# Later operand copies in attention, a later norm of the next rows, and a y part made inside the last down-projection

## The chip, the cores and the metric

The kernel runs on one core of one Trainium2 chip, as one launch. The metric is device time: the median of three timed runs is 3419.69 us (3419.29 to 3424.39). Beside it stands one profiled execution, from which all views come.

## The reference

One layer of a hybrid decoder trunk over 2048 tokens and 16 meta tokens in front, width 1024, all in float32:

```
u      = rms_norm(h) @ w_in + b_in          # 5 parts: attention, RWKV, two gates
y_attn = sliding-window attention (128) with sinks, partial rotary q and k,
         meta tokens as global keys          # 8 query heads, 2 key heads of 64
y_rwkv = RWKV-7 time mixing                  # state update per token, group norm, output gate
h      = h + (g1 * (y_attn @ w_br_attn) + g2 * (y_rwkv @ w_br_rwkv)) @ w_o
f      = rms_norm(h)
h      = h + (silu(f @ w_gate) * (f @ w_up)) @ w_down
out    = rms_norm(h)                         # without the meta tokens
```

## The kernel before

A float32 operand is split in two parts, the first of which ScalarE writes by a copy and the second of which VectorE writes by a subtraction (`chunk`, `split_of`, `Acts`, `Ys.make`); a product is three matmuls on the parts (`mm3`), 128 x 512 each. All TensorE work is of this kind or small matmuls of the two mixers.

The tokens are worked in four blocks of 512. `phase_a(b)` norms a block and makes 37 chunks of the input projection in the order of a list `ORDER`; the chunks go to DRAM (`po` to `proj_d` and `gate_d`). `phase_c(b)` takes a block through the two branch products (`pb`, from the mixers' results `y`, eight parts `ya`), the output product (`ph_o`), a norm, the feed-forward products (`pg`, `pu`, then `ph_d` with `mg_g`) and the final norm, which `finished(t, hf)` does for each of eight pieces of the last down-projection (`ph_d_l`). The program's order is phase A of all blocks, then phase C of all blocks.

Between the products the mixers run: `tick()` (L1016) steps generators, one of attention (`attn(ti)`, L914, 16 tiles of 128 tokens) and up to two of the RWKV units (i, j); each product yields its estimated time, and a tick is due for each third of 4 us of it, an attention step in each third tick. Before phase C of block b the main loop ticks until all mixers' work of the block is in the program (`open_`, L1047).

In an attention tile, q, k and their rotary partners `qr`, `kr` are loaded, GpSimd multiplies by cosine and sine and adds (L934 to L936 for q, L883 to L885 for k: tiles `q`, `kl`), `set_keys` copies the keys on ScalarE to `kw` (L873) and subtracts on VectorE, and `parts(g)` does the same for the queries, `qs` (L944, L945). Scores are `psS`, probabilities go through `pp` and `ptt` to `py`. GpSimd also runs the recurrence of an RWKV unit, 31 pairs of rows `pr` and `xv` (L761, L763), and the power of each norm (`rstd_end`, L232); SyncE fetches `lt` and `xv` for a unit and all weights `wr`.

What sets the order. TensorE's rows stand strictly in the program's order. On ScalarE, VectorE, GpSimd and SyncE a scheduler chooses among the rows of a window by an estimated timeline; `HA`, `HV` issue with high priority, and `late(r)` fixes row r behind the row that was written before it on its engine. A tile takes a buffer of its tag when one comes free: `ld` has 4 buffers (loads `tg`, `yl`, outputs `po`), `act` 8, `tmp` 2, `h` 1 (the block's rows `h`, or the next rows `x`).

In `phase_a`, `rows_of(b + 1)` (L338) at `ORDER[20]` loads the next block's rows `x` and norms them: Squares `jk`, sums `ss_a`, then products. In `phase_c`, `Ys(b)` gives the parts of `y`; the first use, `y[0]`, makes all eight (load `yl`, copy and subtraction `ya`).

Of the kernel before, what the change touches and what calls it, by code (L numbers as in the profile page):

```python
# [21 lines left out]
AF = mybir.ActivationFunctionType  # L22
ALU = mybir.AluOpType
# [4 lines left out]
P = 128  # L28
# [4 lines left out]
NB = SEQ // TB  # L33
# [9 lines left out]
ORDER = [6, 7, 8, 9, 10, 11, 4, 5, 0, 1, 2, 3] + list(range(12, 37))  # L43
# [35 lines left out]
def layer(ctx, tc, x, meta, w_in, w_br, w_o, w_gate, w_up, w_down, w2a, a2, g2, vecs, sinks, gfin,  # L79
          consts, rope, out):  # L80
    nc = tc.nc
    V, A, G, S = nc.vector, nc.scalar, nc.gpsimd, nc.sync
# [20 lines left out]
    def late(r):  # L103

        tc.keep_in_program_order(r)
        return r
# [70 lines left out]
    mhalf = cp.tile([P, 8], F32, name="mhalf")  # L177
# [24 lines left out]
                    return f(*p, **k)  # L202
            return g

    HA, HV = High(A), High(V)


    def chunk(src, name, pin=False):
# [14 lines left out]
        T.matmul(ps, lh, rl, start=False, stop=False)  # L223
        T.matmul(ps, ll, rh, start=False, stop=stop)

    def rstd_half(ss, src, rows, hf, junk):
        HA.activation(junk[:rows, :512], src[:, hf * 512:(hf + 1) * 512], AF.Square, accum_out=ss[:rows, hf:hf + 1])

    def rstd_end(ss, rows):
        HV.tensor_add(ss[:rows, 2:3], ss[:rows, 0:1], ss[:rows, 1:2])  # L230
        HV.tensor_scalar(ss[:rows, 2:3], ss[:rows, 2:3], 1.0 / D, 1e-6, op0=ALU.mult, op1=ALU.add)
        G.tensor_tensor(ss[:rows, 3:4], ss[:rows, 2:3], mhalf[:rows, 0:1], op=ALU.pow)  # L232
        return ss[:rows, 3:4]

    def junk(name):
# [2 lines left out]
    def stat(name):  # L238
        return dn.tile([P, 4], F32, tag="stat", bufs=8, name=f"ss_{name}")

    def rstd_of(src, rows, name, junk):
        ss = stat(name)
        for hf in range(2):
            rstd_half(ss, src, rows, hf, junk)
        return rstd_end(ss, rows)

    class Acts:
# [87 lines left out]
    nxt = [None]  # L335
    emitted = [set() for _ in range(NB)]

    def rows_of(b):  # L338
        rows = []
        xa = dn.tile([P, 4, D], F32, tag="h", name=f"x_{b}")  # L340
        for t in range(4):
            with tc.high_priority():
                late(S.dma_start(xa[:, t], x[b * TB + t * P:b * TB + (t + 1) * P, :]))
        for t in range(4):
            xt = xa[:, t]
            jk = dn.tile([P, 512], F32, tag="tmp", bufs=2, name=f"jk_{b}_{t}")
            r = rstd_of(xt, P, f"a{b}_{t}", jk)
            rows.append((xt[:, :512], xt[:, 512:]))
            HV.tensor_scalar(rows[t][0], rows[t][0], r, None, op0=ALU.mult)
            HA.activation(rows[t][1], rows[t][1], AF.Copy, scale=r)  # L350
        return Acts(rows, "g_mix", f"u{b}")

    def phase_a(b):
        u = nxt[0] or rows_of(b)
        nxt[0] = None
        rest = None
        ws = []
        mid = lambda ci: lambda: ws.append(chunk(w_in[ci], f"in_{b}_{ci}", True))
        for n_, ci in enumerate(ORDER):
            w = ws.pop(0) if ws else chunk(w_in[ci], f"in_{b}_{ci}")  # L360
            if ci == ORDER[20] and b < NB - 1:
                nxt[0] = rows_of(b + 1)
            if ci == ORDER[-1] and b == NB - 1:
                nxt[0] = Ys(0)
            yield from in_chunk(b, ci, u, w, nxt[0] if ci == ORDER[-1] else None, mid(ORDER[n_ + 1]) if b == 0 and n_ < 2 else None)
            if rest:
                rest()
                rest = None
            if b == 0 and ci == ORDER[0]:
                load_rest()  # L370
                meta_norm()
            if b == 0 and ci in META_CH:
                rest = meta_chunk(ci, w)
            else:
                emitted[b].add(ci)
# [29 lines left out]
    class Ys:  # L405
# [14 lines left out]
                self.make()  # L420
            return self.made[k]

        def make(self):
            k = len(self.made)
            if self.early:
                yl = self.early[k // 2][:, k % 2]
            else:
                yl = self.load(dn.tile([P, 1, 512], F32, tag="ld", bufs=4, name=f"yl_{self.b}_{k}"), k, 1)[:, 0]
            a = dn.tile([P, 2, 512], F32R, tag="act", bufs=8, name=f"ya_{self.b}_{k}")
            HA.activation(a[:, 0], yl, AF.Copy)  # L430
            HV.tensor_sub(a[:, 1], yl, f32(a[:, 0]))
            self.made.append(a)

# [6 lines left out]
    def phase_c(b):  # L440
# [6 lines left out]
        for f in range(KT):  # L447
# [24 lines left out]
        rows, st = [], []  # L472
# [41 lines left out]
        sf = []  # L514

        def finished(t, hf):
            if hf == 0:
                sf.append(stat(f"o{b}_{t}"))
            rstd_half(sf[t], h[:, t], P, hf, junk(f"o{b}_{t}_{hf}"))
            if hf:  # L520
                r = rstd_end(sf[t], P)
                for q, e in ((0, S), (1, A)):
                    c = slice(512 * q, 512 * q + 512)
                    if t < 3 and q == 0:
                        HA.activation(h[:, t, c], h[:, t, c], AF.Copy, scale=r)
# [340 lines left out]
    kw = cp.tile([P, 2, 2, 272], F32R, name="kw")  # L866
    MC = slice(P, P + NM)

    def set_keys(k, cols):
        for g in range(2):  # L870
            gb = slice(64 * g, 64 * g + 64)
            for d in (gb, slice(64 - 64 * g, 128 - 64 * g)):
                A.activation(kw[d, g, 0, cols], k[gb], AF.Copy)  # L873
                V.tensor_sub(kw[d, g, 1, cols], k[gb], f32(kw[gb, g, 0, cols]))

    vzs = [cp.tile([P, 3, 64], F32, name=f"vz{q}") for q in range(2)]
# [4 lines left out]
    def roped(o, src, rot, cs, w, name):  # L881

        G.tensor_mul(src, src, cs[:, 0])  # L883
        G.tensor_mul(rot, rot, cs[:, 1])
        G.tensor_add(o, src, rot)  # L885
# [28 lines left out]
    def attn(ti):  # L914
# [7 lines left out]
        q = mx.tile([P, 4, P], F32, tag="q", bufs=1, name=f"q_{ti}")  # L922
# [12 lines left out]
        G.tensor_mul(qr, qr, b4(1))  # L935
        G.tensor_add(q, q, qr)  # L936
        roped(kl[:, 0], kl[:, 0], kr[:, 0], cs, P, ti)
        set_keys(kl[:, 0], own)

        def parts(g):  # L940

            gb, ob = slice(64 * g, 64 * g + 64), slice(64 - 64 * g, 128 - 64 * g)
            qs = mx.tile([P, 4, P], F32R, tag="q0", bufs=1, name=f"qs_{ti}_{g}")
            A.activation(qs[gb], q[gb], AF.Copy)  # L944
            V.tensor_sub(qs[ob], q[gb], f32(qs[gb]))  # L945
            return qs

        qs = parts(0)
# [6 lines left out]
        for g in range(2):  # L955
            gb = slice(64 * g, 64 * g + 64)
# [89 lines left out]
    def open_(b):  # L1046
        return (any(u[3] <= b for u in units) or any((i or 0) // 2 <= b for i, _ in todo_r)  # L1047
                or any((t or 0) // 4 <= b for t in todo_a))

    credit = 0.0  # L1050
    for ph, b in [("a", b) for b in range(NB)] + [("c", b) for b in range(NB)]:
        while ph == "c" and open_(b):
            tick()
        for us in (phase_a if ph == "a" else phase_c)(b):
            credit += us
            while credit >= STEP / TURNS:
                credit -= STEP / TURNS
                tick()
# [119 lines left out]
```

## Time and profile before

| | us |
|---|---|
| median of 3 timed runs | 3419.69 |
| profiled execution, its own time | 3412.06 |
| its span | 3410.3 |
| TensorE busy (share of the span) | 3263.3 (96%) |
| VectorE busy | 1929.6 (57%) |
| ScalarE busy | 1499.4 (44%) |
| GpSimd busy | 1004.8 (29%) |

The mean granted clock of TensorE is 0.984 of full speed. The page's chain of work that ended last is PE 46%, issue 20%, POOL 20%, DMA 7%: where TensorE waits, the chain often runs through GpSimd's recurrence rows and the loads between them. Busy time of the other engines matters only where TensorE waits for one of them; the table of waits and the timelines at those places show where.

### The profile page before, as it was taken

The numbers are of one execution on the slowest core, as the hardware profiler recorded it, in microseconds if no ns is written. First come the engines' busy times: TensorE is split into PE (matmuls) and PEld (weight loads), VectorE is DVE, ScalarE is ACT, GpSimd is POOL, SyncE is SP. The second block draws the span as 40 slices with busy tenths as digits, with TensorE's granted clock in tenths as the row PEclk, the third lists the DMA queues.
The fourth block names the chain that finished last, engine by engine and source line by source line (L and its number), as shares of the span: only waits on it lengthen the run. The fifth ranks groups of instructions, "written<-read, shape, count | busy, mean of one in ns | idle before, by whom it ended". The sixth has DMA issues, their size and how long they took to land.

```text
span 3410.3 us, 47506 instructions
## 1 busy us (share of the span) xinstructions
PE 3263.3 (96%) x16909; PEld 2682.7 (79%) x16909; DVE 1929.6 (57%) x3860; ACT 1499.4 (44%) x3101; POOL 1004.8 (29%) x2290
## 2 busy tenths in 40 slices
PE   8999999999999989999989899999989999999999
PEld 6887778887778777778868788887777888778887
DVE  3344445554544775656667656657655555764455
ACT  4455456554544564445443533434353333432222
POOL 0133333343333343333343244334333341100000
PEclk9999999999999999999989999999999999999999
DMA  4544444454544433333244333335332332522222
GB/s 144 160 144 129 161 133 134 140 157 133 163 131 139 142 103 103 97 91 102 85 139 151 95 102 101 90 98 168 122 95 85 102 94 90 196 96 94 98 99 99
DMA packets 227027, 409.50 MB, mean 120 GB/s; under 512 B 61829, under 2 KB 120581, under 8 KB 226790
## 3 DMA queue, kind: packets, MB, share of 16 engines
q1 hardware_dynamic: 192854, 356.98, 34.5%
q10 hardware_dynamic: 32352, 47.31, 4.0%
q8 instruction: 133, 2.18, 0.3%
q0 software_dynamic: 1584, 2.18, 0.2%
q14 instruction: 104, 0.85, 0.1%
HBM read 346.29 MB, written 60.04 MB: 119 GB/s over the span
## 4 chain that ended last, share of the span: by engine, by line
PE 46%; issue 20%; POOL 20%; DMA 7%; DVE 4%; ACT 2%; SPq 1%; POOLq 0%; ACTq 0%; DVEq 0%
PE pi L93 15%; POOL pr L761 9%; POOL xv L763 8%; PE pg L93 7%; PE pu L93 7%; PE ph_d L93 5%; PE ch L93 2%; PE pb L93 1%; PE ph_o L93 1%; PE py L93 1%; DMA lt<-lt_d 1%; DMA wr_in<-in_w_in 1%; DMA xt_d<-xv 1%; DVE h L202 1%; PE ph_d_l L93 1%
## 5 line engine op out<-in xcount | busy, mean ns | idle before, releaser
L93 PE MATMUL pi<-act_u,wh_in 128*128 128x512 f32 x2368 | 764.1, 404 | 2.3 <-DVE act_u L202 2.1
L761 POOL TENSOR_TENSOR pr<-xv,lt 128x124 f32<-128x124 f32 (+30 forms) x992 | 398.1, 401 | 584.6 <-DMA lt<-lt_d 468.9
L93 PEld LDWEIGHTS pi<-act_u,wh_in 128*128 128x128 f32 x2368 | 425.3, 190 | 83.2 <-issue 5.7
L93 PE MATMUL pi<-act_u,wl_in 128*128 128x512 f32 x1184 | 465.6, 393 | 0.6 <-DVE wl_in L202 0.6
L93 PE MATMUL pg<-act_f,wh_g 128*128 128x512 f32 x1408 | 453.6, 403 | 7.2 <-DVE act_f L202 7.1
L93 PE MATMUL pu<-act_f,wh_u 128*128 128x512 f32 x1408 | 446.7, 398 | 0.0
L93 PE MATMUL ph_d<-wh_d,mg_g 128*128 128x512 f32 x1280 | 428.4, 399 | 16.4 <-DVE th L202 13.6
L763 POOL TENSOR_TENSOR xv<-xv,pr 128x124 f32<-128x124 f32 (+30 forms) x992 | 380.9, 384 | 76.5
L93 PEld LDWEIGHTS pg<-act_f,wh_g 128*128 128x128 f32 x1408 | 256.5, 190 | 57.5 <-DVE act_f L202 9.8
L93 PEld LDWEIGHTS pu<-act_f,wh_u 128*128 128x128 f32 x1408 | 257.5, 189 | 50.3 <-issue 1.5
L93 PEld LDWEIGHTS ph_d<-wh_d,mg_g 128*128 128x128 f32 x1280 | 241.7, 189 | 69.8 <-DVE th L202 15.2
L202 DVE TENSOR_TENSOR wl_in<-wr_in,wh_in 128x1024 fp32r<-128x1024 f32 x148 | 187.0, 1264 | 184.4 <-PE pi L93 126.8
L93 PE MATMUL pg<-act_f,wl_g 128*128 128x512 f32 x704 | 277.6, 394 | 0.0
L93 PE MATMUL pu<-act_f,wl_u 128*128 128x512 f32 x704 | 275.8, 392 | 0.0
L93 PEld LDWEIGHTS pi<-act_u,wl_in 128*128 128x128 f32 x1184 | 223.4, 189 | 51.0 <-DVE wl_in L202 1.0
L93 PE MATMUL ph_d<-wl_d,mg_g 128*128 128x512 f32 x640 | 250.4, 391 | 0.0
L850 POOL TENSOR_TENSOR gst<-gst,mhalf 128x4 f32<-128x4 f32 x32 | 36.1, 1128 | 707.2 <-DVE gst L849 656.8
L202 DVE SCALAR_TENSOR_TENSOR h<-ph_d,h 128x512 f32<-128x512 f32 x320 | 216.5, 685 | 49.1 <-PE ph_d L93 48.1
L202 ACT ACTIVATE wh_g<-wr_g 128x1024 fp32r<-128x1024 f32 x88 | 93.3, 1060 | 220.3 <-PE ph_d L93 81.5
L202 ACT ACTIVATE wh_in<-wr_in 128x1024 fp32r<-128x1024 f32 x148 | 155.8, 1053 | 56.1 <-DMA wr_in<-in_w_in 47.5
L202 DVE TENSOR_TENSOR wl_d<-wr_d,wh_d 128x1024 fp32r<-128x1024 f32 x80 | 99.3, 1242 | 133.1 <-PE pg L93 53.6
L202 DVE TENSOR_TENSOR wl_u<-wr_u,wh_u 128x1024 fp32r<-128x1024 f32 x88 | 108.4, 1232 | 115.5 <-issue 54.2
(358 smaller groups left out, 5940.3 us busy)
## 6 DMA issues: line engine op xcount, KB each, us to landing
wr_in<-in_w_in SPq DMA_DIRECT2D x148, 512.0 KB, 3.8
wr_g<-in_w_gate SPq DMA_DIRECT2D x88, 512.0 KB, 3.6
wr_u<-in_w_up SPq DMA_DIRECT2D x88, 512.0 KB, 3.4
wr_d<-in_w_down SPq DMA_DIRECT2D x80, 512.0 KB, 3.3
proj_d<-po ACTq DMA_DIRECT2D x84, 256.0 KB, 2.5
gate_d<-po ACTq DMA_DIRECT2D x64, 256.0 KB, 2.2
lt<-lt_d SPq DMA_DIRECT2D x32, 512.0 KB
wr_br<-in_w_br SPq DMA_DIRECT2D x32, 512.0 KB, 5.1
```

The lines of the kernel that those rows point to most:

```text
L93: r = f(*p, **k)
L202: return f(*p, **k)
L761: G.tensor_mul(pr[:, :, :n_], xv[:, :, r:r + 1].to_broadcast([P, 4, n_]), lt[:, r, r + 1:].unsqueeze(1).to_broadcast([P, 4, n_]))
L763: G.tensor_add(xv[:, :, r + 1:], xv[:, :, r + 1:], pr[:, :, :n_])
L850: G.tensor_tensor(st[:, 3], st[:, 2], mhalf[:, 0:4], op=ALU.pow)
```

## The change

1. `HG` is added: the power in `rstd_end` is issued on GpSimd with high priority.
2. In `attn`, two yields stand ahead of `set_keys`, so that a tile takes 19 steps instead of 17; the copies to `kw` and `qs` are fixed with `late`.
3. `rows_of` is split: `rows_in` issues the loads of `x` at `ORDER[20]` as before, the norm comes at `ORDER[28]`, its Squares fixed with `late` except for block 0.
4. In `finished`, at piece (2, 1) of blocks 0 to 2, the mixers of block b + 1 are first settled (the ticks that the main loop would make next), then `Ys(b + 1)` is made and the first part of it, its copy fixed with `late`. The other seven parts are made where they were, at `y[0]`.
5. `settle` is the loop that stood in the main program.

The core of the diff:

```
-        G.tensor_tensor(ss[:rows, 3:4], ss[:rows, 2:3], mhalf[:rows, 0:1], op=ALU.pow)
+        HG.tensor_tensor(ss[:rows, 3:4], ss[:rows, 2:3], mhalf[:rows, 0:1], op=ALU.pow)
...
-    def rows_of(b):
-        rows = []
+    def rows_in(b):
         xa = dn.tile([P, 4, D], F32, tag="h", name=f"x_{b}")
         for t in range(4):
             with tc.high_priority():
                 late(S.dma_start(xa[:, t], x[b * TB + t * P:b * TB + (t + 1) * P, :]))
+        return xa
+
+    def rows_of(b, xa):
+        rows = []
...
-            r = rstd_of(xt, P, f"a{b}_{t}", jk)
+            r = rstd_of(xt, P, f"a{b}_{t}", jk, b > 0)
...
             if ci == ORDER[20] and b < NB - 1:
-                nxt[0] = rows_of(b + 1)
+                xa = rows_in(b + 1)
+            if ci == ORDER[28] and b < NB - 1:
+                nxt[0] = rows_of(b + 1, xa)
...
-            HA.activation(a[:, 0], yl, AF.Copy)
+            r = HA.activation(a[:, 0], yl, AF.Copy)
+            if pin:
+                late(r)
...
         def finished(t, hf):
+            if b < NB - 1 and (t, hf) == (2, 1):
+                settle(b + 1)
+                nxt[0] = Ys(b + 1)
+                nxt[0].make(True)
...
-                A.activation(kw[d, g, 0, cols], k[gb], AF.Copy)
+                late(A.activation(kw[d, g, 0, cols], k[gb], AF.Copy))
...
         roped(kl[:, 0], kl[:, 0], kr[:, 0], cs, P, ti)
+        for _ in range(2):
+            yield
         set_keys(kl[:, 0], own)
...
-            A.activation(qs[gb], q[gb], AF.Copy)
+            late(A.activation(qs[gb], q[gb], AF.Copy))
...
     credit = 0.0
     for ph, b in [("a", b) for b in range(NB)] + [("c", b) for b in range(NB)]:
-        while ph == "c" and open_(b):
-            tick()
+        if ph == "c":
+            settle(b)
```

On TensorE the two programs differ only in where the attention matmuls stand. The rows below are those of three places; names end in buffer numbers, which differ between the programs.

**ScalarE at attention tile 14.** `kw` are the key copies, `ptt` the probabilities of the tile before that `py` reads, `wh_d0` and `wh_g` first parts of weights, `rkv`, `kn` and `tw` rows of an RWKV unit. Before:

```order
L991 ACTIVATE ptt_13_1_144_14992<-pp_13_1_144_14987 128x512
L824 ACTIVATE rd_119<-ch_3_1_2_15004 64x64 x2
L873 ACTIVATE kw_126<-kl_14_15092 64x128 x4
L991 ACTIVATE ptt_13_1_0_15033<-pp_13_1_0_15028 128x512
L202 ACTIVATE wh_d0_11_0_15214<-wr_d0_11_0_15212 128x1024
L202 ACTIVATE mg_g0_10_15042<-th_0_10_15038 128x512
L1003 ACTIVATE q_13_14128<-py_13_14730 128x512
```

Now:

```order
L1006 ACTIVATE ptt_13_1_0_16484<-pp_13_1_0_16479 128x512
L563 ACTIVATE rkv_4_1_16467<-rp_4_1_16468,omix_96 128x256 x3
L650 ACTIVATE kn_4_1_16510<-rkv_4_1_16467,nkk_98 128x256
L202 ACTIVATE wh_g_0_19_16663<-wr_g_0_19_16661 128x1024
L886 ACTIVATE kw_126<-kl_14_16541 64x128 x4
L651 ACTIVATE tw_4_1_16511<-kn_4_1_16510 128x256
L1018 ACTIVATE q_13_15465<-py_13_16168 128x512
```

The key copies stand some eight feed-forward chunks later, behind both `ptt` of tile 13 instead of between them, and what follows them is an RWKV row and the tile's result.

**GpSimd at attention tile 2**, where the queries' rows `q_2` stand among the recurrence of unit (0, 0), of which `pr_0_0_n` and `xv` with it are step n. Before:

```order
L761 TENSOR_TENSOR pr_0_0_2_2824<-xv_0_0_2816,lt_0_0_2814 128x4x29
L763 TENSOR_TENSOR xv_0_0_2816<-xv_0_0_2816,pr_0_0_2_2824 128x4x29
L934 TENSOR_TENSOR q_2_2923<-q_2_2923,cs_2_2921 128x512
L761 TENSOR_TENSOR pr_0_0_3_2827<-xv_0_0_2816,lt_0_0_2814 128x4x28
L936 TENSOR_TENSOR q_2_2923<-q_2_2923,qr_2_2924 128x512
L763 TENSOR_TENSOR xv_0_0_2816<-xv_0_0_2816,pr_0_0_3_2827 128x4x28
```

Now:

```order
L776 TENSOR_TENSOR xv_0_0_2797<-xv_0_0_2797,pr_0_0_28_2883 128x4x3
L774 TENSOR_TENSOR pr_0_0_29_2886<-xv_0_0_2797,lt_0_0_2795 128x4x2
L776 TENSOR_TENSOR xv_0_0_2797<-xv_0_0_2797,pr_0_0_29_2886 128x4x2
L947 TENSOR_TENSOR q_2_3062<-q_2_3062,cs_2_3060 128x512
L774 TENSOR_TENSOR pr_0_0_30_2889<-xv_0_0_2797,lt_0_0_2795 128x4
L949 TENSOR_TENSOR q_2_3062<-q_2_3062,qr_2_3063 128x512
L776 TENSOR_TENSOR xv_0_0_2797<-xv_0_0_2797,pr_0_0_30_2889 128x4
```

The queries' product and sum moved from step 2 of the recurrence to its last two steps.

**The y parts: ScalarE at the end of block 0's feed-forward part.** `ya_1` are the parts of block 1, `mg_g0_21` the operand that `ph_d` waits for, `wh_d0` weights of the down-projection, `rd` a row of an RWKV unit. Before:

```order
L202 ACTIVATE th_0_21_17462<-pg_0_21_17389 128x512
L202 ACTIVATE wh_d0_21_1_17521<-wr_d0_21_1_17519 128x1024
L202 ACTIVATE ya_1_0_17787<-yl_1_0_17785 128x512
L202 ACTIVATE ya_1_1_17792<-yl_1_1_17790 128x512
L824 ACTIVATE rd_119<-ch_4_0_2_17445 64x64 x2
L202 ACTIVATE ya_1_2_17797<-yl_1_2_17795 128x512
L202 ACTIVATE ya_1_3_17802<-yl_1_3_17800 128x512
L202 ACTIVATE wh_d0_l_0_17573<-wr_d0_l_0_17571 128x1024
L202 ACTIVATE mg_g0_21_17466<-th_0_21_17462 128x512
```

Now:

```order
L202 ACTIVATE th_0_21_17271<-pg_0_21_17178 128x512
L202 ACTIVATE wh_d0_21_1_17352<-wr_d0_21_1_17350 128x1024
L837 ACTIVATE rd_119<-ch_4_0_2_17254 64x64 x2
L202 ACTIVATE wh_d0_l_0_17404<-wr_d0_l_0_17402 128x1024
L202 ACTIVATE mg_g0_21_17275<-th_0_21_17271 128x512
```

No y part stands ahead of `mg_g0_21` any more. The eight now stand behind the Squares of piece (2, 0) of the final norm and later.

**SyncE at the end of block 2**, with the loads `yl_3` of block 3's parts from the third on, the outputs `out_0` of block 2, weights `wr`, and gates `tg`. Before:

```order
L415 DMA yl_3_2_28826<-y_d_77 128x512
L415 DMA yl_3_3_28831<-y_d_77 128x512
L212 DMA wr_d2_l_1_28694<-in_w_down 128x1024
L415 DMA yl_3_4_28836<-y_d_77 128x512
L415 DMA yl_3_5_28841<-y_d_77 128x512
L212 DMA wr_br_3_0_28810<-in_w_br 128x1024
L415 DMA yl_3_6_28846<-y_d_77 128x512
L512 DMA gft_2_28667<-in_gfin 128x1024
L212 DMA wr_br_3_1_28894<-in_w_br 128x1024
L861 DMA y_d_77<-tl_7_3_28682 128x256
L415 DMA yl_3_7_28851<-y_d_77 128x512
```

Now:

```order
L542 DMA out_0<-h_2_23510 128x512
L422 DMA yl_3_2_28826<-y_d_77 128x512
L212 DMA wr_br_3_2_28938<-in_w_br 128x1024
L542 DMA out_0<-h_2_23510 128x512
L422 DMA yl_3_3_28831<-y_d_77 128x512
L212 DMA wr_br_3_3_28982<-in_w_br 128x1024
L422 DMA yl_3_4_28836<-y_d_77 128x512
L422 DMA yl_3_5_28841<-y_d_77 128x512
L542 DMA out_0<-h_2_23510 128x512 x2
```

The loads that stood among the last weights of the down-projection now stand behind the outputs of the block.

## Rows read from the trace of the kernel before

**Rows 1.** The page's busy times: us, share of the span, instructions.

```profile
PE 3263.3 (96%) x16909; PEld 2682.7 (79%) x16909; DVE 1929.6 (57%) x3860; ACT 1499.4 (44%) x3101; POOL 1004.8 (29%) x2290
```

**Rows 2.** TensorE's waits, whole span: us in total, times, longest us.

```profile
PE ch L93 <- ACT yt L836: 23.0, 12, 4.9
PE py L93 <- ACT ptt L991: 15.6, 6, 5.1
PE ph_d L93 <- DVE th L202: 13.6, 5, 10.4
PE pt_f L93 <- DVE f L202: 11.6, 4, 8.8
...
PE psS L93 <- DVE qs L945: 9.1, 5, 2.1
```

**Rows 3.** Timeline, GpSimd and ScalarE, tile 14: start, us, instruction, [idle before <-releaser].

```profile
1500.70 0.44 POOL L884 TENSOR_TENSOR kr<-kr,cs 128x128 f32<-128x128 f32 x1 [6.63 <-DMA kr<-proj_d]
...
1501.71 1.29 ACT L873 ACTIVATE kw<-kl 64x128 fp32r<-64x128 f32 x4 [11.21 <-POOL kl L885]
```

**Rows 4.** Timeline of GpSimd, then ScalarE, at tile 4.

```profile
488.73 0.25 POOL L763 TENSOR_TENSOR xv<-xv,pr 128x36 f32<-128x36 f32 x1
...
490.73 0.31 ACT L873 ACTIVATE kw<-kl 64x128 fp32r<-64x128 f32 x1 [9.95 <-POOL kl L885]
```

**Rows 5.** TensorE's waits from 420 to 432, 484 to 497, 700 to 720.

```profile
PE ch L93 <- ACT yt L836: 4.0, 1, 4.0
...
PE py L93 <- ACT ptt L991: 2.5, 1, 2.5
...
PE psS L93 <- DVE qs L945: 2.0, 1, 2.0
```

**Rows 6.** Windows: busy us (instructions) by engine, TensorE's clock, DMA share, GB/s.

```profile
492.00:496.00 4.00, 3.44 (x5) 1.66 (x6) 1.78 (x4) 2.81 (x6) 3.08 (x10) 0.57 0.56 163
1502.00:1510.00 8.00, 6.46 (x15) 3.87 (x16) 3.92 (x8) 3.71 (x8) 0.00 (x0) 0.57 0.36 110
1741.00:1755.00 14.00, 5.30 (x13) 4.14 (x14) 5.44 (x10) 3.99 (x6) 0.73 (x2) 0.51 0.39 122
```

**Rows 7.** Timeline, GpSimd at tiles 2, 4, 10, ScalarE at 2, 10.

```profile
335.60 0.21 POOL L763 TENSOR_TENSOR xv<-xv,pr 128x8 f32<-128x8 f32 x1
...
503.19 1.29 POOL L934 TENSOR_TENSOR q<-q,cs 128x512 f32<-128x512 f32 x1 [6.84 <-DMA q<-proj_d]
...
1233.86 0.32 POOL L763 TENSOR_TENSOR xv<-xv,pr 128x72 f32<-128x72 f32 x1
...
324.57 0.51 ACT L637 ACTIVATE kn<-rkv,nkk 128x256 f32<-128x256 f32 x1
...
1220.42 0.45 ACT L824 ACTIVATE rd<-ch 64x64 f32<-64x64 f32 x2
```

**Rows 8.** Timeline of ScalarE at the norm of block 1's rows.

```profile
420.80 0.63 ACT L202 ACTIVATE jk<-x 128x512 f32<-128x512 f32 x1 [5.84 <-DMA x<-in_x]
```

**Rows 9.** Timeline of ScalarE at the end of block 0's feed-forward part.

```profile
1747.69 0.63 ACT L202 ACTIVATE ya<-yl 128x512 fp32r<-128x512 f32 x1 [12.24 <-DMA yl<-y_d]
```

**Rows 10.** Timeline of SyncE's queue, ScalarE, VectorE, TensorE at block 2's end.

```profile
2937.49 0.33 SPq L415 DMA_DIRECT2D yl<-y_d  x1
...
2944.83 0.34 SPq L529 DMA_DIRECT2D out<-h  x1
...
2920.71 0.63 ACT L202 ACTIVATE ya<-yl 128x512 fp32r<-128x512 f32 x1 [3.19 <-DMA yl<-y_d]
...
2941.16 0.63 ACT L202 ACTIVATE ya<-yl 128x512 fp32r<-128x512 f32 x1 [1.15 <-DMA yl<-y_d]
...
2941.82 0.69 DVE L202 TENSOR_TENSOR ya<-yl,ya 128x512 fp32r<-128x512 f32 x1 [0.55 <-ACT ya L202]
...
2948.16 0.62 PE L93 MATMUL pb<-ya,wh_br 128*128 128x512 f32 x2
```

**Rows 11.** Timeline of GpSimd in block 2's second norm.

```profile
2497.62 0.40 POOL L761 TENSOR_TENSOR pr<-xv,lt 128x124 f32<-128x124 f32 x1 [10.74 <-DMA lt<-lt_d]
```

More of the change, by code (lines that the diff above doesn't have):

```diff
@@ L203, in __getattr__ @@
             return g
-    HA, HV = High(A), High(V)
+    HA, HV, HG = High(A), High(V), High(G)
     def chunk(src, name, pin=False):
@@ L224, in mm3, with rstd_half @@
         T.matmul(ps, ll, rh, start=False, stop=stop)
-    def rstd_half(ss, src, rows, hf, junk):
-        HA.activation(junk[:rows, :512], src[:, hf * 512:(hf + 1) * 512], AF.Square, accum_out=ss[:rows, hf:hf + 1])
+    def rstd_half(ss, src, rows, hf, junk, pin=False):
+        r = HA.activation(junk[:rows, :512], src[:, hf * 512:(hf + 1) * 512], AF.Square, accum_out=ss[:rows, hf:hf + 1])
+        if pin:
+            late(r)
     def rstd_end(ss, rows):
@@ L239, in stat, with rstd_of @@
         return dn.tile([P, 4], F32, tag="stat", bufs=8, name=f"ss_{name}")
-    def rstd_of(src, rows, name, junk):
+    def rstd_of(src, rows, name, junk, pin=False):
         ss = stat(name)
         for hf in range(2):
-            rstd_half(ss, src, rows, hf, junk)
+            rstd_half(ss, src, rows, hf, junk, pin)
         return rstd_end(ss, rows)
@@ L353, in phase_a @@
     def phase_a(b):
-        u = nxt[0] or rows_of(b)
+        u = nxt[0] or rows_of(b, rows_in(b))
         nxt[0] = None
@@ L421, in __getitem__, with make @@
             return self.made[k]
-        def make(self):
+        def make(self, pin=False):
             k = len(self.made)
@@ L429, in make @@
             a = dn.tile([P, 2, 512], F32R, tag="act", bufs=8, name=f"ya_{self.b}_{k}")
-            HA.activation(a[:, 0], yl, AF.Copy)
+            r = HA.activation(a[:, 0], yl, AF.Copy)
+            if pin:
+                late(r)
             HV.tensor_sub(a[:, 1], yl, f32(a[:, 0]))
@@ L1048, in open_, with settle @@
                 or any((t or 0) // 4 <= b for t in todo_a))
+    def settle(b):
+        while open_(b):
+            tick()
     credit = 0.0
     for ph, b in [("a", b) for b in range(NB)] + [("c", b) for b in range(NB)]:
-        while ph == "c" and open_(b):
-            tick()
+        if ph == "c":
+            settle(b)
         for us in (phase_a if ph == "a" else phase_c)(b):
```

## The prediction

> **What bounds the kernel now.** I read first the page's busy times, then the table of what TensorE waited for, then the stretches around the long waits on the engine that was late. TensorE is busy for 3263.3 us of a span of 3410.3 [rows 1], so only some 147 us of idle time and the stretches at the lower clock can be won; all else on TensorE is the same products in the same order in both kernels, but for the 615 attention matmuls, which now come later. The waits are many and small [rows 2]: the reader should see there the four kinds that the change speaks to (`py` for `ptt`, `psS` for `qs`, `ph_d` for `th`, `pt_f` for `f`) and one that it doesn't, `ch` for `yt`, 23.0 us, most of which hangs on SyncE and GpSimd. After a wait of 2 us or more the granted clock often falls to its lower level, 1.2 GHz, for some 3.4 or 6.8 us, which the windows show as means of 0.51 to 0.57 [rows 6].
>
> **Part 1, the attention operands behind GpSimd.** Rows: ScalarE stands in front of the key copies `kw` for 11.2 us until GpSimd has written `kl` [rows 3]; the `ptt` that `py` needs is queued right behind, as the order shows, and TensorE loses 5.1 us, the longest of its `py` waits [rows 2]. At tile 4 it is 9.95 us on ScalarE [rows 4] and 2.5 on TensorE [rows 5]. GpSimd is late either because its adds stand among the recurrence's rows [rows 4] or because `kr` landed late [rows 3]. Of the six `py` waits, 15.6 us in sum, five are of this kind, 0.4 to 5.1 us, together 14.5. Of the `psS` waits, 9.1 [rows 2], I leave out 2.0 that stands beside the norm of the next rows [rows 5]: 7.1. Behind five of these waits the clock is at half: in the longest stretch 8 us at 0.57, which is 3.4 lost, in the four others some 4 us like the first, 1.7 each [rows 6]. That is 10.2, and as TensorE is busy for 0.81 to 0.86 of them, 8.7 us. Gain if all goes: 14.5 + 7.1 + 8.7 = 30.3.
>
> It doesn't all go. Two steps of the attention generator later also move every step after them, and the queries' rotation meets another place of the recurrence. The order shows it at tile 2: `q_2`'s two GpSimd rows stood behind recurrence step 2, now behind steps 29 and 30. On the times of before, step 29 ends at 335.8, and with the two rows (1.29 for the product at tile 4, and the sum as long) the queries are ready at about 338.5, while ScalarE gets to the `qs_2` copy, now fixed in place, at about 325 [rows 7]: a wait of some 13 us, with `po` and `wh_in` of the projection behind it. At tile 10 the rows stand behind step 13, whose `xv` ends at 1234.2; ScalarE is there at 1220.9 [rows 7], some 15 us early, with `wh_o`, `mg_m` and a `yt` that `ch` needs behind it. From the pairs above (11.2 us on ScalarE cost 5.1, 9.95 cost 2.5) I take 5 us each. At tiles 4, 5 and 7 the same count gives waits of 2.5 to 5.5 us, for which I take 1 each. Residue 13 (bounds 0, if the later TensorE takes the wait up, and 22). **Net -17.3.**
>
> **Part 2, the next rows' norm.** Before, ScalarE waited 5.84 us for `x` to land, in front of the exponentials `sm` and, further on, a `yt` [rows 8]; TensorE lost 4.0 at `ch` [rows 5] and some 1.7 by the clock, as in the first window [rows 6], and the 2.0 at `psS` of tile 6 [rows 5]: 7.7. The loads keep their place and the Squares come eight chunks later, so that wait goes. New: for block 2 the first GpSimd power now stands behind recurrence step 22, at 489.0 on the times of before [rows 4], and the products of `x` with it are in front of ScalarE and VectorE from about 482. That is 7 us, the size of the waits that cost 2.5; I take 3 (bounds 0 and 5). **Net -4.7.**
>
> **Part 3, the y parts.** Before, ScalarE stands 12.24 us in front of `ya_1_2`, because `yl` was issued late on SyncE behind `xv` [rows 9]; `mg_g`, without which `ph_d` can't start, is two rows further on, and TensorE loses 10.4, the longest of the `ph_d` waits [rows 2]; of the 3.2 in the four others I give the two further block ends 2.0. With TensorE busy for 5.3 of 14 us at 0.51 [rows 6], the clock costs 2.6. In the new order no `ya` stands in front of `mg_g`: **-15.0**.
>
> The price is paid at the three block ends themselves. Before, the eight parts came one by one over the 20 us and more ahead of `pb` (behind block 2 one at 2920.71, the last at 2941.16 [rows 10]), under the down-projection's products; now the first is made at (2, 1) of the last down-projection, two of its pieces (2.8 us) ahead of `pb`. The four `ld` buffers hold `yl_0`, `yl_1` and two `tg`, so `yl_2` waits for `ya_0`'s subtraction, `yl_4` for `ya_2`'s, `yl_6` for the first `mt`: a chain of loads, while TensorE asks for a part each 0.69 us. From issue to ScalarE's start the last load took 3.7 us (2937.49 to 2941.16); 0.63 on ScalarE and 0.69 on VectorE follow [rows 10]: 5.0 for a round. Behind block 2, put on before's times: `ya_0` takes the slot of VectorE's last `ya`, done at 2942.5; `yl_3` goes out behind the second `out` of SyncE (2944.83), and its part is there at 2950.2; `mt` ends at 2951.6, `yl_6` and `yl_7` follow, and part 7 is there at 2957.4, where TensorE used it at 2948.16 [rows 10]: +9.3. Behind block 1 the same count gives +10.4; behind block 0, where tile 15's `kr` loads stand on SyncE too, +8 to +12 less what a wait of `pq` for `tq` there takes up, so 8.3. Together 28.0; nothing behind `pb` waits long enough before to give this back. Each of the three has two or three gaps of 2 to 5 us, as those behind which the clock fell; of the 1.7 to 3.4 us that such a fall cost [rows 6] I take 1.5 a block, since part of it falls in the gaps: 4.5. **Net +17.4** (bounds of the price: 12, with one exposed round a block, and 52).
>
> A rule of the Trainium skill speaks for less. The rows have 3.7 us from issue to use for one load of 256 KB [rows 10]. The page "DMA: Bandwidth & Descriptors", section "Anatomy of one DMA — SWDGE (gpsimd) path", gives a fixed 2.0 us and the bytes at 436 GB/s, an estimate of 2.6 us here. By it a round is 3.9 and the three blocks cost some 10 us less, and the whole sum would be about -14. The rows decide, since they are the very loads, and from SyncE's queue, while the page's fit is for GpSimd's.
>
> **Part 4, the powers first on GpSimd.** `pt_f` lost 8.8 us because a power stood behind a recurrence product that waited 10.74 us for `lt` [rows 2, 11]. High priority should mend this, but in the new order the same power still stands behind the same row there (`ss_f2_3` behind `pr_6_3_0`); the powers that moved did so beside recurrence rows of 0.4 us. **0** (bounds -14, if they came first, and +1).
>
> Attention's later place puts tiles 14 and 15 into block 1's branch and output products: +1 (0 to 4). SyncE's `xv` loads, behind which weights and so `yt` are late, stand where they were in 28 of 33 units: 0.
>
> **Sum**: -17.3 - 4.7 - 15.0 + 32.5 + 0 + 1 = -3.5, against the profiled execution's 3412.06: 3408.5. The median of the timed runs, 3419.69, lies 7.6 above that execution, which I leave as it is: **3416**.
>
> **The rivals.** (1) *The chain of y parts is mostly covered.* For it: VectorE and ScalarE are nearly idle there, and one load took 3.7 us, a part of which may lie beside another's; only the first round would show, some 5 us a block, 15 + 1 for the clock instead of 32.5. Against: one buffer less anywhere renews the chain. Time 3416 - 16 = 3400. The skill's rule above points this way. (2) *SyncE's queue makes it longer, and the kernel slower.* The `yl` loads now stand behind `out` issues, each of which waits for GpSimd's product with `gft`; behind block 0 GpSimd also has tile 15's rotation to do in front of these. If a second round in each block starts only behind the last `out`, a block costs 5 to 7 us more, +18, and the time is 3434. It decides from 11 us a block on; against it, those GpSimd rows are short. (3) *The powers do come first*, since places in an order on an engine are only where they stand, and `lt` may now land earlier: -14, 3402. The change not doing what it says in part 4 is in the forecast.
>
> **How the numbers follow.** A measurement of this kernel can tell about 0.2%, 6.8 us, from no change: faster is under 3412.9, slower over 3426.5. Forecast (about -3.5, 3403 to 3425 by the bounds of part 1): 0.45, of it 0.16 faster, 0.27 same, 0.02 slower. Rival 1: 0.23, faster. Rival 2: 0.28, of it 0.27 slower, 0.01 same. Rival 3: 0.04, faster. Faster 0.43, same 0.28, slower 0.29. Cases of both signs hold much, so the range reaches to both: 3394 (rival 1 with half of part 1's residue gone) to 3437 (rival 2 with 3 us for the attention rows); the forecast's own is 3403 to 3425.
>
> **What would show it.** Right: `py` for `ptt` under 4 us and `ph_d` for `th` under 2; `psS` for `qs`, or what stands behind `qs` on ScalarE, late at tiles 2 and 10; `pb` waiting for `ya`, a new row of the waits with 20 to 30 us in nine or so pieces at three places; ScalarE no longer waiting for `x`; the 8.8 at `pt_f` still there. Wrong: `pb` waits under 12 us (rival 1) or over 40 (rival 2), a `pt_f` wait gone (rival 3), or a new wait at a place that I have not named, above all at `ch`, whose `yt` shares ScalarE with all that is moved.

## The result: slower by 0.8%

The changed kernel takes 3446.2 us, the median of four timed runs (3445.12 to 3452.38), beside 3420.83 us of the kernel before on the same chip: a ratio of 1.0076, with a 95% interval of 1.0059 to 1.0094, so 20 to 32 us slower. Forecast were 3416 us and a range of 3394 to 3437. The time lies beyond the range, on the side of the second rival, but, as the trace of block 2's end below shows, not by that rival's way.

The page of the changed kernel begins with these lines (busy us, share of the span, instructions), which answer to [rows 1].

```profile
span 3450.6 us, 47495 instructions
...
PE 3282.8 (95%) x16909; PEld 2694.4 (78%) x16909; DVE 1932.1 (56%) x3860; ACT 1500.7 (43%) x3101; POOL 992.1 (29%) x2290
```

The span is 40.3 us longer than that of before. TensorE does the same 16909 products, and is busy for 19.5 us more (3282.8 against 3263.3): that is the lower clock, granted at 0.975 in the mean where it was 0.984. The other 20.8 us are idle time (167.8 against 147.0). The timed medians differ by 25 us only; two single executions of one kernel can differ by some 8 us, as one of the experiments shows.

What TensorE waited for, over the whole span of the changed kernel (us in total, times, longest us), to be read beside [rows 2]:

```profile
PE ch L93 <- ACT yt L849: 31.2, 13, 7.3
PE pt_f L93 <- DVE f L202: 16.0, 6, 10.1
PE ch L93 <- DVE ud L842: 13.9, 3, 7.2
PE pb L93 <- ACT ya L202: 12.6, 10, 3.5
...
PE pb L93 <- DVE ya L202: 7.4, 7, 3.4
...
PE ph_o L93 <- DVE mt L202: 6.1, 2, 5.5
PE ch L93 <- ACT rd L837: 6.1, 2, 4.0
PE ph_d L93 <- DVE th L202: 3.2, 2, 2.6
...
PE ch_None L93 <- DVE ud L842: 3.1, 1, 3.1
```

Of the four kinds of wait that the change speaks to, three went: `py` for `ptt` (15.6 us) and `psS` for `qs` (9.1) have no row any more, and `ph_d` for `th` fell from 13.6 to 3.2. The fourth, `pt_f` for `f`, is still there, as forecast. In their place stand `pb` for `ya`, 20.0 us in 17 pieces, and waits of the RWKV chain `ch`: for `yt` 31.2 instead of 23.0, and for `ud` 17.0 and `rd` 6.1, which had no row before. The prediction had named a new wait at `ch` as a sign that it was wrong.

On ScalarE itself (what it waited for; before, then the changed kernel) one of the two waits for GpSimd went, and the other stayed:

```profile
ACT kw L873 <- POOL kl L885: 67.6, 15, 11.2
...
ACT qs L944 <- POOL q L936: 53.6, 12, 9.4
```

```profile
ACT qs L959 <- POOL q L949: 54.2, 11, 12.1
...
ACT kw L886 <- POOL kl L898: 6.9, 3, 3.3
```

### The profile page after: what moved, and what is told of

Read it like the earlier page. It is cut to its first block, busy times and chain, and to the rows that moved or that the text cites. A ratio compares the mean times of both kernels' runs of the same rounds, so it can differ in the third digit from the quotient of the medians.

```text
span 3450.6 us, 47495 instructions
## 1 busy us (share of the span) xinstructions
PE 3282.8 (95%) x16909; PEld 2694.4 (78%) x16909; DVE 1932.1 (56%) x3860; ACT 1500.7 (43%) x3101; POOL 992.1 (29%) x2290
## 4 chain that ended last, share of the span: by engine, by line
PE 31%; issue 16%; POOL 12%; DMA 3%; DVE 3%; ACT 1%; SPq 0%; POOLq 0%; ACTq 0%; DVEq 0%
PE pg L93 8%; PE pu L93 7%; PE ph_d L93 7%; POOL pr L774 5%; POOL xv L776 5%; PE ph_o L93 2%; PE pb L93 2%; PE ch L93 1%; PE ph_o_l L93 1%; DVE h L202 1%; DMA lt<-lt_d 0%; DMA wr_g<-in_w_gate 0%; DMA wr_d<-in_w_down 0%; PE ph_d_l L93 0%; PE py L93 0%
## 5 line engine op out<-in xcount | busy, mean ns | idle before, releaser
L774 POOL TENSOR_TENSOR pr<-xv,lt 128x124 f32<-128x124 f32 (+30 forms) x992 | 381.1, 384 | 603.3 <-DMA lt<-lt_d 470.6
L93 PE MATMUL pb<-ya,wh_br 128*128 128x512 f32 x512 | 175.7, 421 | 22.2 <-ACT ya L202 12.6
```

Of the source, the lines that this page charges most:

```text
L93: r = f(*p, **k)
L774: G.tensor_mul(pr[:, :, :n_], xv[:, :, r:r + 1].to_broadcast([P, 4, n_]), lt[:, r, r + 1:].unsqueeze(1).to_broadcast([P, 4, n_]))
```

## The experiments

All ran beside the kernel before on the same chip; the ratio is to its runs of that session (medians of 3415 to 3421 us), with a 95% interval. The last column is worked out from the ratio, at 3419 us.

| kernel | ratio | interval | us against before |
|---|---|---|---|
| the whole change | 1.0076 | 1.0059 to 1.0094 | +26 |
| attention part alone | 1.0054 | 1.0037 to 1.0071 | +18.5 |
| y part alone | 1.0054 | 1.0038 to 1.0069 | +18.5 |
| norm part alone | 0.9988 | 0.9974 to 1.0002 | -4 |
| powers alone | 1.0003 | 0.9991 to 1.0015 | +1 |
| two yields alone | 1.0075 | 1.0057 to 1.0093 | +26 |
| fixed copies alone | 1.0017 | 1.0004 to 1.0030 | +6 |
| copies later, 17 steps | 1.0034 | 1.0021 to 1.0048 | +12 |
| two yields at a tile's end | 1.0016 | 1.0004 to 1.0027 | +5.5 |
| y part at (0, 0) | 1.0004 | 0.9991 to 1.0018 | +1.5 |
| y part spread over eight pieces | 1.0028 | 1.0016 to 1.0040 | +9.5 |
| `xv` loads on GpSimd's queue | 0.9840 | 0.9825 to 0.9854 | -55 |
| that and the attention part | 0.9824 | 0.9803 to 0.9845 | -60 |
| that and the y part | 0.9914 | 0.9898 to 0.9931 | -29 |
| that and the norm part | 0.9813 | 0.9797 to 0.9829 | -64 |
| that, norm, powers and y part at (0, 0) | 0.9849 | 0.9831 to 0.9867 | -52 |
| that and the whole change but its y part | 0.9839 | 0.9819 to 0.9858 | -55 |
| that and the whole change | 0.9907 | 0.9891 to 0.9923 | -32 |

### The four parts, each alone

The attention part (two yields, copies fixed):

```diff
-                A.activation(kw[d, g, 0, cols], k[gb], AF.Copy)
+                late(A.activation(kw[d, g, 0, cols], k[gb], AF.Copy))
...
+        for _ in range(2):
+            yield
         set_keys(kl[:, 0], own)
...
-            A.activation(qs[gb], q[gb], AF.Copy)
+            late(A.activation(qs[gb], q[gb], AF.Copy))
```

> The kernel before with the attention part alone: two yields ahead of the key copies, and the copies to kw and qs fixed in place. Theory A (the y parts at the block ends make the kernel slower, the attention part still helps as forecast): 17 us faster than before, since the waits of py for ptt (14.5 us) and of psS for qs (7.1) with their half clock (8.7) go but for 13. Theory B (ScalarE's wait for GpSimd only moves from kw to qs, where the trace of after still has 54 us of it, and TensorE then waits at ch): within 5 us of before, with qs waits of ScalarE of 50 us and more. Theory C (the attention part is itself the loss): 10 us or more slower.

It is 18.5 us slower (13 to 24 by the interval): theory C. The y part:

```diff
         def finished(t, hf):
+            if b < NB - 1 and (t, hf) == (2, 1):
+                settle(b + 1)
+                nxt[0] = Ys(b + 1)
+                nxt[0].make(True)
```

> The kernel before with the y part alone: at piece (2, 1) of blocks 0 to 2 the mixers settled and the first y part made and fixed there. The attention stays as before. Theory A and B alike, from the drift of the two traces at the three block ends (+14 to +16 each, less the 11 won at the wait of ph_d for th): 25 to 32 us slower. If my prediction's sizes held (28 and 4.5 of clock less 15.0): 17 us slower. A rival, that the loss of after lies with the attention's later place: within 7 us of before.

Also 18.5 us slower, close to the size that I had predicted for it (+17.4), and less than the drift of the traces had made me expect. The norm part, with the Squares fixed as in the change:

```diff
             if ci == ORDER[20] and b < NB - 1:
-                nxt[0] = rows_of(b + 1)
+                xa = rows_in(b + 1)
+            if ci == ORDER[28] and b < NB - 1:
+                nxt[0] = rows_of(b + 1, xa)
```

> The kernel before with the later norm of the next rows alone. The prediction's step: 4.7 us faster, the 5.8 us wait of ScalarE for x gone, 7 us of waiting for the first power in block 2 new. Rival: the Squares fixed in place hold ScalarE elsewhere, 0 to 8 us slower.

It is 4 us faster, with an interval that just includes no change. The powers:

```diff
-        G.tensor_tensor(ss[:rows, 3:4], ss[:rows, 2:3], mhalf[:rows, 0:1], op=ALU.pow)
+        HG.tensor_tensor(ss[:rows, 3:4], ss[:rows, 2:3], mhalf[:rows, 0:1], op=ALU.pow)
```

> The kernel before with the powers' priority alone; only GpSimd's order differs from that of before. The prediction's step: 0, the pt_f wait of 8 to 10 us in block 2 still there. Rival: powers come ahead of recurrence rows where it counts, 5 to 14 us faster.

No difference, and for a plain reason: without the other parts not one row of any engine changes its place, so this is the kernel before once more. It is the measure of what single traces can tell: its profiled execution has a span of 3418.1 us for 3410.3, and runs of before in one session went from 3404 to 3425 us. The four parts sum to +34 us, the whole is +26.

In the attention part's own trace TensorE waits as follows (rows of its table of waits):

```profile
PE ch L93 <- ACT rd L824: 13.9, 3, 6.2
PE ch L93 <- DVE ud L829: 13.2, 3, 6.4
...
PE py L93 <- ACT ptt L993: 6.2, 2, 3.2
...
PE ch_None L93 <- DVE ud L829: 3.5, 1, 3.5
```

What left `py` and `psS` came back on the chain: for `rd` and `ud` 30.6 us that were not there before. (Its waits for `yt`, 23.7 us, are as before; the rise of these in the whole change belongs mostly to the y part, as shown further down.) The place with the longest wait for `ud`, tile 5, reads as follows in the changed kernel (SyncE's queue; GpSimd; ScalarE; VectorE; then what TensorE waited for between 670 and 690 us):

```profile
662.36 0.33 SPq L941 DMA_DIRECT2D kl<-proj_d  x1
672.66 0.33 SPq L770 DMA_DIRECT2D xv<-in_consts  x1
673.10 0.38 SPq L937 DMA_DIRECT2D q<-proj_d  x1
```

```profile
676.26 1.25 POOL L947 TENSOR_TENSOR q<-q,cs 128x512 f32<-128x512 f32 x1 [5.32 <-DMA q<-proj_d]
677.59 1.26 POOL L949 TENSOR_TENSOR q<-q,qr 128x512 f32<-128x512 f32 x1
```

```profile
678.88 0.63 ACT L959 ACTIVATE qs<-q 64x512 fp32r<-64x512 f32 x1 [12.05 <-POOL q L949]
```

```profile
679.55 0.69 DVE L960 TENSOR_TENSOR qs<-q,qs 64x512 fp32r<-64x512 f32 x1 [15.55 <-ACT qs L959]
...
681.62 0.34 DVE L842 TENSOR_SCALAR ud<-ch,rnb 128x128 f32<-128x128 f32 x1
```

```profile
PE ch L93 <- DVE ud L842: 7.2, 1, 7.2
```

SyncE issues nothing for 10 us, since the load of `xv`, the start values of the next recurrence, may only go when the recurrence before has been written out; the queries' load stands right behind. ScalarE then waits 12.05 us in its fixed place, and VectorE's `qs` subtraction, behind it the chain's `ud`, waits with it. At this tile ScalarE did not wait for the queries at all before.

### Yields, fixed copies, or cadence

The first run has the two yields of the diff above without `late`, the second the two `late` without the yields. The third has both, and two yields less behind the queries' copy, so that a tile keeps its 17 steps:

```diff
         qs = parts(0)
-        for _ in range(2):
-            yield
```

The fourth has two yields at the end of a tile and nothing else:

```diff
         A.dma_start(y_d[0:4, :, ti * P:(ti + 1) * P].rearrange("f p t -> p f t"), q)
+        for _ in range(2):
+            yield
```

> The kernel before with the two yields ahead of the key copies and nothing else; no copy is fixed. Theory P (the cadence: a tile takes 19 steps for 17, all later attention work meets other rows of the recurrence and of ScalarE): as much slower as both edits together, 13 to 24 us. Theory Q (the copies fixed in place hold ScalarE's other rows while GpSimd is late): 0 to 10 us faster than before.

> The kernel before with the copies to kw and qs fixed in place and no yields; TensorE's rows stand as in before. Theory P: within 5 us of before. Theory Q: 8 to 20 us slower.

> The attention part with the two yields moved, not added: two ahead of the key copies, and those behind the first queries' copy taken out, so that a tile keeps its 17 steps; copies fixed. Both operands' copies come two steps behind the rotation, the scores follow at once. Theory P: no loss, and the waits for kw go, 3 to 12 us faster than before. Theory Q: 8 to 20 us slower, as with the pins alone. Rival R (the scores then wait for the copies, since nothing is left between): psS for qs over 12 us in all, 5 to 10 us slower.

> The kernel before with two yields at the very end of an attention tile, after its result: nothing inside a tile moves, but the next tile starts two steps later, so a tile takes 19 steps as in the change. Theory P (the cadence costs: all later attention rows meet other rows of the recurrence, the weights and the mixers): 13 to 30 us slower than before, as the two yields ahead of the key copies (+24). Theory U (the yields cost by their place, the rotation's rows being written before them and the copies after): within 6 us of before.

The yields cost it, +26 us by themselves, and the fixed copies little, +6: theory Q falls. But the cadence alone, the same 19 steps with the yields at the end, costs only +5.5, so theory P, as I had put it, falls too: it matters where in the tile the yields stand. Without the fixed copies the yields don't even help ScalarE: in that run it waits 65.7 us in front of `kw` and 52.5 in front of `qs`, as before (67.6 and 53.6); that the scheduler draws the copies forward again is my reading. With 17 steps rival R holds: the scores come at once behind the copies, and `psS` waits for `qs` for 33.1 us in ten pieces, where it was 9.1 us. The time, +12, is a little over R's 5 to 10; by the time alone theory Q would fit as well, and the wait decides.

### The y part's place

```diff
-            if b < NB - 1 and (t, hf) == (2, 1):
+            if b < NB - 1 and (t, hf) == (0, 0):
```

> The kernel before with the y part alone, as in the run of it alone, but at piece (0, 0) of the last down-projection, five pieces (6.9 us) earlier. Theory S (the chain of loads starts too late for its three rounds of 5 us): the three block ends cost 15 to 20 us less than at (2, 1), so within 6 us of before, pb waits for ya under 8 us. Theory T (fixing the copy or settling early costs, not the place): still 13 us or more slower.

One part behind each piece:

```diff
+            if b < NB - 1:
+                if (t, hf) == (0, 0):
+                    settle(b + 1)
+                    nxt[0] = Ys(b + 1)
+                nxt[0].make(True)
```

> The kernel before with the y part alone, but one of the eight y parts made and fixed behind each of the eight pieces of the last down-projection, from (0, 0) on. Theory S (the parts come too late and three rounds of loads in a chain are exposed): at the block ends nothing is lost but the last part, some 2 us each, the 11 us wait of ph_d for th gone: 5 to 13 us faster than before. Rival: the fixed copies wait for their loads on ScalarE and hold the Squares and the weights' copies: 0 to 15 us slower.

Five pieces earlier, 6.9 us, the part costs nothing in sum, 17 us less than at (2, 1): theory S. What it wins at `ph_d` for `th` (13.6 to 1.6 us) and its prices cancel. `pb` still waits, 8.3 us for `ya` where it was 21.9 at (2, 1), as two rows of that run show:

```profile
PE pb L93 <- DVE ya L202: 5.4, 3, 3.3
...
PE pb L93 <- ACT ya L202: 2.9, 2, 1.6
```

Spread over the pieces it is worse, +9.5: in that trace `pb` waits 17.2 us for `ya`, up to 4.9 us in one piece. The time lies in the rival's 0 to 15, but not by its way: ScalarE's table of waits in that run has no row for `yl`. That parts which each wait for a piece come too late again is my reading and not shown.

### SyncE's stands at `xv`

The chains behind many of the waits, in both kernels, ended at SyncE in front of `xv`. One line takes them away, by issuing the same 33 loads from GpSimd, which needs them:

```diff
-        S.dma_start(xv.rearrange("p c i -> p (c i)"), consts[:, slice(*_CC["x0"])])
+        G.dma_start(xv.rearrange("p c i -> p (c i)"), consts[:, slice(*_CC["x0"])])
```

> The kernel before with the load of xv's start values issued on GpSimd's queue instead of SyncE's; TensorE's order is that of before. SyncE stands 5 to 17 us in front of each of these 33 loads until the unit before is done, with weight loads behind. If that is what the ch waits for yt (23 us) and some of the waits of ph_o for h hang on, as the chains of both traces say: 15 to 30 us faster with the half clock behind them. If GpSimd then stands in the load's place with rotations and powers behind: 0 to 10 us slower.

It is 55 us faster, more than all waits that I had put down to it. Little else moves: TensorE's order is the same, and by names 23 of VectorE's 3860 rows and 70 of GpSimd's 2290 change their place. The stand on SyncE before and in the changed kernel, and what GpSimd has in its place (rows of the tables of waits):

```profile
SPq L757 <- DMA xt_d<-xv: 341.5, 30, 17.1
```

```profile
SPq L770 <- DMA xt_d<-xv: 345.0, 31, 16.6
```

```profile
POOL xv L757 <- DMA xt_d<-xv: 72.0, 31, 6.3
```

and two rows of what TensorE then waits for, 23.0 and 13.6 us before:

```profile
PE ch L93 <- ACT yt L836: 3.8, 5, 2.4
...
PE ph_d L93 <- DVE th L202: 1.0, 2, 0.5
```

Idle time falls to 108.6 us (3360.5 less 3251.9 busy), and the clock's share with it: TensorE is busy for 11.4 us less than before. The long wait of `ph_d` for `th`, 10.4 us, is gone without any y part being moved: the `yl` loads for which ScalarE stood there [rows 9] had been issued at 1743.93, right behind an `xv` for which SyncE had stood since 1731.6 (SyncE's queue before):

```profile
1731.25 0.33 SPq L212 DMA_DIRECT2D wr_d_l<-in_w_down  x1
1743.55 0.33 SPq L757 DMA_DIRECT2D xv<-in_consts  x1
1743.93 0.90 SPq L415 DMA_DIRECT2D yl<-y_d  x2
```

With these stands away, the parts were run again, each by its own diff above on top of this line: the attention part, the y part, the norm part, then norm, powers and the y part at (0, 0), then the whole change without and with its y part.

> The attention part alone (two yields, copies fixed), put on the kernel whose xv loads are issued on GpSimd's queue (3362.6 us). Theory V (the part loses because SyncE's stands at xv catch the queries' and weights' loads at the new places, as the chains at tiles 0, 5 and 10 say): with those stands gone it is 0 to 17 us faster than 3362.6. Theory W (it loses on ScalarE and VectorE themselves: the qs copy and subtraction, still 50 us behind GpSimd, now stand in front of rows of the RWKV chain): 12 to 25 us slower than 3362.6, as much as on the kernel before.

> The y part alone, with the xv loads on GpSimd's queue. If the wait of ph_d for th (11 us and its half clock, 13 to 15 in all) that the part removes was made by an xv stand, the part has only its price left here: 28 to 35 us over 3362.6, so 3391 to 3398. If the part's price also came from these stands: within 10 us of 3362.6.

> The later norm of the next rows alone, with the xv loads on GpSimd's queue: 3 to 8 us under 3362.6 if its gain is its own, within 2 us of it if it was the xv stands that made x land late.

> The later norm, the powers' priority and the first y part at piece (0, 0), with the xv loads on GpSimd's queue, attention as before. Each part was between -4 and +1 on the kernel before: 3355 to 3365 us. If the wait of ph_d for th, which the y part removes, was made by the xv stands, the y part has nothing to win here and costs its block ends: 3365 to 3375.

> The whole change without its y part, with the xv loads on GpSimd's queue: attention part, norm and powers. If the parts add (norm -6.7 and attention -1.8 against 3362.6): 3354 us; if the attention part's gain of kw waits grows once the norm is out of its way, 3345 to 3352; if they meet each other, 3358 to 3368.

> The whole change with the xv loads issued on GpSimd's queue. Theory V: the y part's some 18 us are left and 4 are won by the norm, 3362 to 3378 us. Theory W: 3380 to 3395 us, the loss of the whole change (26 us) as on the kernel before.

The attention part, 18.5 us slower on the kernel before, is here 0.16% or some 5 us faster (3360.82 for 3362.55 in the medians; the two intervals overlap): theory V. The y part costs here 0.74% or 25 us, more than before: with the `th` wait already gone it has only its price. That price is below the expected 28 to 35, which fits a part of it, too, having come from the stands. The whole change is 23 us slower on this base as well: its 3388.5 us lie in the range that theory W gave, but by the y part, since without it the same kernel takes 3359.87. The norm part wins 9 us by the ratios and 6.7 by the medians; with the attention part it is not faster still (0.9839, 3359.87 us), though these intervals overlap as well. The early y part, neutral before, costs here too: with the norm and the powers it is 3369.19 us, 13 over the norm part alone.

The fastest kernel is the one before with the `xv` loads on GpSimd's queue and the later norm: **3355.85 us**, 0.9813 of before, faster than both kernels of this case.

## Why the prediction was wrong, step by step

**Part 1, -17.3: wrong, +18.5 found.** The gain side was right: all of the 21.6 us of `py` and `psS` waits went in the changed kernel (in the part's own trace 6.2 of them are left). The residue of 13 us was the term that failed, with the 0 for SyncE's `xv` loads: by the forecast's own gain of 30.3 the residue came to 49. Two steps lie behind it.

First, I counted how long ScalarE would wait at tiles 2, 10, 4, 5 and 7 from GpSimd's rows alone, on the times of before. The places were good, the sizes not: at tile 2 ScalarE waited 9.3 us for 13, at tile 10 5.6 for 15, and TensorE lost 3.1 and 5.5 for 5 each; but at tile 5, put down as 1 us, it lost 7.2, because the queries' load was itself late. And the price was counted without the clock, though the gain was counted with it.

Second, and this is the larger one, the sentence on SyncE: that its `xv` loads "stand where they were in 28 of 33 units: 0". The stands are as long as before, 345.0 for 341.5 us. But the attention's loads and matmuls moved against them, so other work now stands behind each. The runs show that the part's loss needs these stands: on a SyncE without them the same part costs nothing, some 24 us less. They are not the whole of it: of the 30.6 us that `ch` waited for `ud` and `rd` in the part's own trace, 17.8 are left on that base (at tile 5 3.8 for 6.4), while the waits of `py` and `psS`, 25.4 us on that base, fall to 2.0 with the part. Which stand catches which row has been followed at tile 5 only, and why two yields ahead of the copies cost 20 us more than two at the tile's end is left open.

**Part 2, -4.7: right**, -4 alone (-9 to +1), and 7 to 9 on the better base. In its own trace ScalarE's 5.84 us for `x` and the 4.0 of `ch` at that place are gone; of the 2.0 at `psS` 1.4 are left.

**Part 3, +17.4: right in sum**, +18.5 alone (13 to 24), and right in its mechanism at the block ends; but the sum also holds a wait of another kind, so a part of the agreement is luck. At the end of block 2 in the changed kernel (SyncE's queue; ScalarE; VectorE; TensorE), beside [rows 10]:

```profile
2969.87 0.32 SPq L422 DMA_DIRECT2D yl<-y_d  x1
...
2982.14 1.05 SPq L422 DMA_DIRECT2D yl<-y_d  x2
```

```profile
2973.16 0.63 ACT L202 ACTIVATE ya<-yl 128x512 fp32r<-128x512 f32 x1 [1.97 <-DMA yl<-y_d]
...
2986.50 1.22 ACT L202 ACTIVATE ya<-yl 128x512 fp32r<-128x512 f32 x2 [2.92 <-DMA yl<-y_d]
```

```profile
2981.43 0.68 DVE L202 SCALAR_TENSOR_TENSOR mt<-tg,pb 128x512 f32<-128x512 f32 x1
```

```profile
2970.34 0.61 PE L93 MATMUL pb<-ya,wh_br 128*128 128x512 f32 x2
...
2987.18 1.52 PE L93 MATMUL pb<-ya,wh_br 128*128 128x512 f32 x2 [1.60 <-ACT ya L202]
...
2988.93 1.05 PE L93 MATMUL pb<-ya,wh_br 128*128 128x512 f32 x2
```

The rounds are there, and the last two loads are issued at 2982.14, when the first `mt` ends. TensorE gets to part 7 at 2988.93, 18.6 us after its first `pb`; before it took 5.8 (2942.38 to 2948.16). That is 12.8 us for my 9.3 and 1.5 of clock. The chain was sized well: from issue to ScalarE's start the rows shown have 3.3 us (2969.87 to 2973.16) and 4.4 (2982.14 to 2986.50) for the 3.7 taken. The trace so stays nearer to [rows 10] than to the estimate of 2.6 us that I had worked out from the Trainium skill's page "DMA: Bandwidth & Descriptors", section "Anatomy of one DMA — SWDGE (gpsimd) path". The clock was not sized well: the windows around the three block ends in the changed kernel, then before (length; busy us of TensorE, its weight loads, VectorE, ScalarE and GpSimd; TensorE's clock, DMA share, GB/s) are

```profile
1765.00:1800.00 35.00, 26.39 (x135) 18.42 (x135) 27.06 (x57) 17.07 (x37) 7.07 (x8) 0.85 0.72 240
2380.00:2412.00 32.00, 20.10 (x53) 13.10 (x54) 21.60 (x34) 16.27 (x35) 8.32 (x11) 0.68 0.70 234
2960.00:2995.00 35.00, 26.88 (x93) 18.30 (x92) 25.21 (x41) 16.71 (x33) 6.99 (x7) 0.80 0.75 250
```

```profile
1765.00:1800.00 35.00, 31.08 (x172) 25.70 (x171) 28.73 (x64) 17.73 (x42) 8.60 (x8) 0.90 0.62 209
2360.00:2392.00 32.00, 27.47 (x129) 23.19 (x130) 24.85 (x46) 15.59 (x33) 7.68 (x8) 0.89 0.73 245
2935.00:2970.00 35.00, 33.18 (x146) 26.81 (x145) 28.17 (x44) 14.81 (x27) 7.68 (x7) 1.00 0.82 280
```

The part of the clock that was not granted is 22.5 us (35 at 0.15, 32 at 0.32, 35 at 0.20) for 7.0 before: 15.5, some of it in idle time, where I took 4.5. So waits of 20.0 us in pieces of 0.2 to 3.5 us cost nearly as much again by the clock; at block 2 no piece was longer than 1.8 us, and yet only 0.80 of the clock was granted. Rival 2's mechanism, a second round behind the last `out`, is not what is seen: the last loads follow `mt`, as in the forecast.

What the part's sum did not have stands some 80 us behind block 0's end. SyncE's queue before, then SyncE's queue and ScalarE in the changed kernel:

```profile
1830.11 0.33 SPq L212 DMA_DIRECT2D wr_br<-in_w_br  x1
...
1842.75 0.33 SPq L757 DMA_DIRECT2D xv<-in_consts  x1
```

```profile
1832.31 0.33 SPq L212 DMA_DIRECT2D wr_o<-in_w_o  x1
1848.11 0.33 SPq L770 DMA_DIRECT2D xv<-in_consts  x1
...
1849.09 0.33 SPq L212 DMA_DIRECT2D wr_br<-in_w_br  x1
```

```profile
1853.50 1.06 ACT L202 ACTIVATE wh_br<-wr_br 128x1024 fp32r<-128x1024 f32 x1 [13.42 <-DMA wr_br<-in_w_br]
1854.58 0.27 ACT L849 ACTIVATE yt<-ch 64x128 f32<-64x128 f32 x1
```

One `xv` load that stood behind a branch weight `wr_br` now stands in front of it; ScalarE waits 13.42 us for that weight, with `yt` behind it, and `ch` loses 7.3 us, its longest wait for `yt`. It is the y part's: in that part's own run, whose order on TensorE is that of before, the wait is 7.9 us, at (0, 0) 9.6 and spread 9.9; in the attention part's run no wait for `yt` is over 4.6, and in the y part's on the base without the stands none over 2.3. So this is one of the five units, of the 33, that the prediction's 0 for SyncE passed over. Without the stands the part's price is 25 us, against some 33 with them (18.5, and the 15.0 forecast as its gain; at `th` its own run won 12.8).

**Part 4, 0: right.** The wait of `pt_f` is still there, 10.1 us; the priority alone moves no row.

**Attention's later place, +1: right for TensorE.** Where tile 15 now runs, from 1732 to 1910 us before and from 1746 to 1937 in the attention part's own trace, TensorE is idle for 26.4 us before and for 25.6 there, at a clock of 0.91 and 0.93: nothing is lost.

**The rivals and the range.** None of the three described what happened. Rival 1 took VectorE and ScalarE as nearly idle at the block ends, which is misread: in the window at block 2's end before, VectorE is busy for 28.17 of 35 us and ScalarE for 14.81. The forecast's own bounds for part 1 ended at a residue of 22 us; 49 would have been needed. None of the bounds came from rows that would newly stand behind SyncE's old waits.

## What to carry to other kernels

A long stand of one queue that costs little is not harmless: everything that is moved can come to stand behind it, so take it away first, and judge other moves afterwards; here one changed word won 55 us and turned an 18 us loss into nothing. Count an operand as late from its load on, not from the engine that last writes it, and give every new wait the price of the clock as well. A chain of loads through few buffers needs its first step as many rounds ahead as it has rounds; pinning its start close to the use exposes it.

## What the runs showed that was not expected

GpSimd waited 72.0 us for the 33 loads that it now issues, in place of SyncE's 341.5, and TensorE's waits behind GpSimd hardly changed by it: `py` for `ptt` and `psS` for `qs` are 25.4 us in sum for 24.7. Why it costs so little is not shown; that GpSimd waits for the same recurrence's `lt` in any case (468.9 us before, 509.0 with the loads on its queue) speaks for it only in part, since that wait did not shrink. And the same rows in the same order gave spans of 3410.3 and 3418.1 us, so a difference of 8 us between two traces is not yet one.
